# A hybrid encoder layer on one core: the second softmax's factor on GpSimd, other planned waits in attention, and a gate tile in another stage

## The chip, the cores and the metric

The kernel runs on one core of a Trainium2 chip. Its engines are TensorE (PE for matmuls, PEld for the loading of the stationary operand), the Vector engine (DVE), ScalarE (ACT), GpSimd (POOL) and SyncE (SP), which issues the DMAs. Each works off its own instructions in order and waits for the others on semaphores. The metric is the device time of one execution in microseconds (us). Three runs of the kernel before took 886.32, 886.88 and 886.91 us; the median is 886.88.

## What is computed

One layer (DEPTH is 1) of an encoder over 512 tokens of width 1024, all in float32. Cut to what matters:

```python
h = rms_norm(x, norm1_g[l])
proj = h @ w_in[l]                      # 1024 x 7680
u_pool, aq, ak, av, rq, rf, rb, ri, rg, gate_pre = split_cols(proj)
y_pool = pool_mixer(u_pool, pool_w[l], pool_scale[l])   # windows 2, 4, 8, 16; then a 128x128 map per group
# differential attention, 4 heads, two score maps (c = 0, 1) per head:
s = einsum('bqhcd,bkhcd->bhcqk', q, k) * scale - slopes * abs(qpos - pos)
p = softmax(s, axis=-1)
a = p[:, :, 0] - lam * p[:, :, 1]
y_attn = rms_norm(einsum('bhqk,bkhe->bqhe', a, v), gain) * (1.0 - lambda_init)
y_rec = hgrn2_mixer(rq, rf, rb, ri, rg, ...)            # bidirectional gated recurrence
gates = sigmoid(gate_pre.reshape(B, S, 3, D_MODEL))
merged = (gates[:, :, 0] * (y_pool @ w_up_pool[l]) + gates[:, :, 1] * (y_attn @ w_up_attn[l])
          + gates[:, :, 2] * (y_rec @ w_up_rec[l]))
x = x + merged @ w_out[l]
h2 = rms_norm(x, norm2_g[l])
gu = h2 @ w_ffn_in[l]
x = x + (silu(gu[..., :FFN_HIDDEN]) * gu[..., FFN_HIDDEN:]) @ w_ffn_out[l]
return rms_norm(x, final_norm_g)
```

## The kernel before

Operands of the large products are split in a high and a low part (`whi`, `wlo`; `hT_hi`, `hT_lo`), and a product is three terms: high by high, low by high, high by low. A *job* is one such product, most often of a tile of 128 output columns with all 512 tokens: 24 matmuls of 128x512 in three groups of eight for a column tile of `w_in`, 12 for a column tile of an up projection. For a job the weights are loaded by SP (`raw`), cast on ScalarE (`whi`, L183) and the rest formed on the Vector engine (`wlo`, L184), ahead of time, in three rotating buffers.

The program runs stage by stage. In each, `Pipe.run` interleaves several streams: a stream yields ("w", t) to say that it wants to go on only after t us of planned TensorE time, or ("e", name, t) to wait for an event. The stream of jobs never waits and so fills every gap. This plan fixes the order of TensorE's instructions. On the other engines a scheduler places instructions by its own timing of the program, so their order can change with any edit; each engine then keeps that order on the chip.

The attention stage runs four `att_head` streams, the `pool_windows` stream and the jobs from the queries and keys of attention to the four `pool_job` tiles (u0 to u3), with the first four up tiles of the recurrent branch among them. A head treats four query blocks. `scores(i)` makes two 128x512 score maps on TensorE (tiles `rc<-k,q` and `rc<-l,q`, four matmuls), adds the distances and finds the extreme on the Vector engine (L1056), takes the exponential with its sum on ScalarE (L1058, sums in `zz`), and forms on the Vector engine both reciprocals (`rr`, L1062), the factor `co` = -lam times the first sum over the second (L1064; `nlam` is -lam) and the weighted row `s` (L1066). `turn(i)` transposes that row on TensorE (L98, `tp<-ident,s`) and splits it (`aT_hi` on ScalarE, `aT_lo` on the Vector engine, L1076). After the fourth block come the product with the values (`rc<-aT_hi,va_hi` and so on, 12 matmuls) and `head_norm`: squares on ScalarE, four small products with ones (`tp<-onesD,sqo`), three small steps `mo` on the Vector engine with `rr`, a power on GpSimd (`rso`, L140), a product with `rr` (L667) and four transposes of `rso`. TensorE meets, in this order: scores(0), wait, scores(1), wait, turn(0), wait, scores(2), wait, turn(1), and so on.

`pool_windows` forms the pooled differences of u0 to u3 (`win`, L1159, and `gate`, L1166 and L1168). The next stage runs `pool_mix` (four groups: `dhi` on ScalarE, `dlo` on the Vector engine, L1181, three matmuls `rc<-dhi,pwhi`, `rc<-dlo,pwhi`, `rc<-dhi,pwlo`, an evacuation to `y_arena`), `SplitForms.stream` (sums of parts of h for later products, `gsum`, `ghi`, `glo`), and the jobs: gate tiles 4 and 5 of the recurrent branch (`add_gates((4, 5), "extra")`), its up tiles 4 and 5, gate tiles 6 and 7. A gate job ends with a sigmoid on ScalarE into a tile of `GATE[extra]`; an up job with a product `merged<-mm,gate` (L756).

Of the kernel before, what the change touches and what calls it, by code (L numbers as in the profile page):

```python
# [11 lines left out]
F32 = mybir.dt.float32  # L12
# [3 lines left out]
ALU = mybir.AluOpType  # L16
PSUM = bass.MemoryType.PSUM

P = 128
S = 512  # L20
D = 1024
NB = S // P
# [16 lines left out]
class Pipe:  # L39
# [8 lines left out]
    def mark(self, name):  # L48
        self.events[name] = self.t
# [27 lines left out]
def encoder_kernel(ctx: ExitStack, tc: tile.TileContext, x, norm1_g, w_in, pool_w, pool_scale,  # L77
# [3 lines left out]
    nc = tc.nc  # L81
# [3 lines left out]
    def pool(name, bufs=1, **kw):  # L85
        return tc.tile_pool(name=name, bufs=bufs, **kw)
# [21 lines left out]
    const = ctx.enter_context(pool("const"))  # L108
    wraw = ctx.enter_context(pool("wraw", 2))
    wsp = ctx.enter_context(pool("wsp", 3))  # L110
    small = ctx.enter_context(pool("small", 5))
# [15 lines left out]
    nc.vector.memset(onesD, 1.0 / P)  # L127
    mhalf = const.tile([P, 8], F32, name="mhalf")
    nc.vector.memset(mhalf, -0.5)
    masks = const.tile([P, len(LEVELS), P], U8, name="masks")  # L130
    vcol = const.tile([P, 14], F32, name="vcol")
    gain_a = const.tile([P, 1], F32, name="gain_a")
# [373 lines left out]
    GATE = {}  # L506
# [140 lines left out]
    def head_norm(o_ps, tmp, gain, r0=None, bufs=2):  # L647


        og = tmp.tile([P, S], F32, name="og", bufs=bufs)  # L650
        sq = tmp.tile([P, S], F32, name="sqo", bufs=bufs)
        nc.scalar.activation(out=sq, in_=o_ps, func=AF.Square)
        nc.scalar.activation(out=og, in_=o_ps, func=AF.Copy, scale=gain)
        yield ("w", 1.3)
        sp = bank("tp")
        for b in range(NB):
            mm(sp[:, b:b + 1], sq[:, b * P:(b + 1) * P], onesD, True, True)
        r = small.tile([P, NB], F32, name="rso")
        if r0 is None:
            rsqrt_eps(r, sp[:, 0:NB])  # L660
        else:
            m = small.tile([P, NB], F32, name="mo")
            nc.vector.tensor_tensor(out=m, in0=sp[:, 0:NB], in1=r0, op=ALU.mult)
            nc.vector.tensor_tensor(out=m, in0=m, in1=r0, op=ALU.mult)
            nc.vector.tensor_scalar(out=m, in0=m, scalar1=EPS, scalar2=None, op0=ALU.add)
            pow_mhalf(r, m)
            nc.vector.tensor_tensor(out=r, in0=r, in1=r0, op=ALU.mult)  # L667
        yield ("w", 3.55)
        rb = bank("tp")
        for b in range(NB):  # L670
            transpose(rb[:, b * P:(b + 1) * P], r[:, b:b + 1].to_broadcast([P, P]), ident)
        return og, rb
# [359 lines left out]
    def att_head(h):  # L1032
        if h:
            yield ("e", f"QK{h - 1}", 0.0)
        if h > 1:
            yield ("e", f"AN{h - 2}", 0.0)
        yield ("e", f"AF{h}", 6.0)
        t = att.pop(h)
        at, (vh, vl), aT, y_attn = ATT["at"], ATT["v"], ATT["aT"], ATT["y"]
        strip = ATT["strip"].tile([P, 896], F32, name="strip")  # L1040
        nc.sync.dma_start(out=strip, in_=c_dist[h])
        zz = at.tile([P, NB, 2], F32, name="zz")
        rr = at.tile([P, NB, 2], F32, name="rr")
        probs = {}

        def scores(i):
            bs = slice(i * P, (i + 1) * P)
            mx = small.tile([P, 2], F32, name="mx")
            ex = []
            for c in range(2):  # L1050
                ps = bank("rc")
                mm(ps, t[f"q{c}"][:, bs], t[f"k{c}"], True, False)
                mm(ps, t[f"q{c}"][:, bs], t[f"l{c}"], False, True)
                s = at.tile([P, S], F32, name=f"s{c}")

                nc.vector.tensor_tensor_reduce(out=s, in0=strip[:, 384 - P * i:896 - P * i], in1=ps, scale=1.0,  # L1056
                                               scalar=3.0e38, op0=ALU.add, op1=ALU.min, accum_out=mx[:, c:c + 1])
                nc.scalar.activation(out=s, in_=s, func=AF.Exp, scale=-1.0, bias=mx[:, c:c + 1],  # L1058
                                     accum_out=zz[:, i, c:c + 1])
                ex.append(s)  # L1060

            nc.vector.reciprocal(out=rr[:, i, :], in_=zz[:, i, :])  # L1062
            co = small.tile([P, 1], F32, name="co")
            nc.vector.scalar_tensor_tensor(out=co, in0=zz[:, i, 0:1], scalar=nlam, in1=rr[:, i, 1:2],  # L1064
                                           op0=ALU.mult, op1=ALU.mult)
            nc.vector.scalar_tensor_tensor(out=ex[0], in0=ex[1], scalar=co, in1=ex[0], op0=ALU.mult, op1=ALU.add)  # L1066
            probs[i] = ex[0]

        def turn(i):
            bs = slice(i * P, (i + 1) * P)  # L1070
            p = probs.pop(i)
            pt = bank("tp", (P, NB, P))
            for k in range(NB):
                transpose(pt[:, k, :], p[:, k * P:(k + 1) * P], ident)
            nc.scalar.copy(out=aT[0][:, :, bs], in_=pt)
            nc.vector.tensor_tensor(out=aT[1][:, :, bs], in0=pt, in1=aT[0][:, :, bs].bitcast(F32), op=ALU.subtract)  # L1076

        scores(0)
        for i in range(NB):
            yield ("w", 1.8 + (0.7 if i == 0 else 0.0))  # L1080
            if i + 1 < NB:
                scores(i + 1)
            else:
                mark(f"QK{h}")
            yield ("w", 1.6 + (1.0 if i + h == 0 else 0.0))
            if h and i == 0:
                yield ("e", f"PV{h - 1}", 0.0)
            turn(i)
        mark(f"T{h}")
        yield ("e", "VA", 1.5)  # L1090
        yield ("w", 1.5)
        ps = bank("rc")
        es = slice(h * P, (h + 1) * P)
        terms = [(vh, aT[0]), (vl, aT[0]), (vh, aT[1])]
        for i, (a, r) in enumerate(terms):
            for k in range(NB):
                mm(ps, a[:, k, es], r[:, k, :], i == 0 and k == 0, i == 2 and k == NB - 1)
            yield
        mark(f"PV{h}")
        og, rbp = yield from head_norm(ps, at, gain_a, rr[:, :, 0], 1)  # L1100
        mark(f"AN{h}")
        nc.vector.tensor_tensor(out=og, in0=og, in1=rbp, op=ALU.mult)
        nc.scalar.copy(out=y_attn[0][:, h, :], in_=og)
        nc.vector.tensor_tensor(out=y_attn[1][:, h, :], in0=og, in1=y_attn[0][:, h, :].bitcast(F32),
                                op=ALU.subtract)
# [32 lines left out]
    def add_pool(gs):  # L1138
        for g in gs:
            jobs.add([next(cols["u"])], pool_job(g))  # L1140

    add_pool((0, 1))
    br_rec.add_ups(range(2, 4))
    add_pool((2, 3))
    n_att = len(jobs.jobs)


# [24 lines left out]
    def pool_mix():  # L1172
        w, whi, wlo = POOL["w"], POOL["whi"], POOL["wlo"]
        nc.scalar.copy(out=whi, in_=w)
        nc.vector.tensor_tensor(out=wlo, in0=w, in1=whi.bitcast(F32), op=ALU.subtract)
        for g in range(4):
            yield ("w", 4.0)
            d = POOL[g][:, PAD:PAD + S]
            hi, lo = (POOL["t"].tile([P, S], F32R, name=n) for n in ("dhi", "dlo"))
            nc.scalar.copy(out=hi, in_=d)  # L1180
            nc.vector.tensor_tensor(out=lo, in0=d, in1=hi.bitcast(F32), op=ALU.subtract)  # L1181
            yield ("w", 2.6)
            ps = bank("rc")
            for i, (w_, r) in enumerate(((whi, hi), (whi, lo), (wlo, hi))):
                mm(ps, w_[:, g, :], r, i == 0, i == 2)
            y = POOL["y"]
            nc.scalar.activation(out=y[0][:, g, :], in_=ps, func=AF.Copy, scale=pscale[:, g:g + 1])
            nc.vector.scalar_tensor_tensor(out=y[1][:, g, :], in0=ps, scalar=pscale[:, g:g + 1],
                                           in1=y[0][:, g, :].bitcast(F32), op0=ALU.mult, op1=ALU.subtract)
            if g == 1:  # L1190
                mark("M1")

    br_rec.add_gates((4, 5), "extra")
    br_rec.add_ups((4, 5))
    br_rec.add_gates((6, 7), None, "M1")
    n_forms = len(jobs.jobs)
# [504 lines left out]
    stR.close()  # L1701

    merged.grow(stA.enter_context(pool("mp")))
    ya = stA.enter_context(pool("ya"))
    with ExitStack() as st:
        ap1 = st.enter_context(pool("ap1"))
# [20 lines left out]
    with ExitStack() as st:  # L1727
        pp = st.enter_context(pool("pp"))
        POOL["t"] = st.enter_context(pool("pt3"))
        GATE["extra"] = st.enter_context(pool("gp2", 2))  # L1730
        POOL["w"] = pp.tile([P, 4, P], F32, name="pw")
        POOL["whi"], POOL["wlo"] = (pp.tile([P, 4, P], F32R, name=n) for n in ("pwhi", "pwlo"))
        nc.sync.dma_start(out=POOL["w"], in_=pool_w[0].rearrange("g c d -> c g d"))
        forms = LAST["gforms"].stream(fm, st.enter_context(pool("gwork", 3)))
        pipe.run([pool_mix(), forms, jobs.stream(n_forms - n_att)])
# [95 lines left out]
```

## Time and profile before

| | us |
|---|---|
| profiled execution, device time | 886.27 |
| its span (first to last instruction) | 884.5 |
| Vector engine busy | 664.5 |
| ScalarE busy | 448.4 |
| GpSimd busy | 18.7 |
| start and end of the attention stage's blocks (first `s` row to last) | 220.2 to 329.6 |

A row of the timeline gives the start from the beginning of the span, the duration, the engine, the line of the kernel, the operation, what it writes and reads, its shape and the number of instructions merged in the row; in brackets the idle time of the engine before it and what ended that. A row of windows gives the stretch, its length, the busy time of each engine with its number of instructions, the granted clock of TensorE (1.00 is full), the DMA share and GB/s. A row of groups gives line, engine, operation and tile, then busy time, the mean duration in ns, and idle time before with what ended it.

### The profile page before, as it was taken

The numbers are of one execution on the slowest core, as the hardware profiler recorded it, in microseconds if no ns is written. First come the engines' busy times: TensorE is split into PE (matmuls) and PEld (weight loads), VectorE is DVE, ScalarE is ACT, GpSimd is POOL, SyncE is SP. The second block draws the span as 40 slices with busy tenths as digits, with TensorE's granted clock in tenths as the row PEclk, the third lists the DMA queues.
The fourth block names the chain that finished last, engine by engine and source line by source line (L and its number), as shares of the span: only waits on it lengthen the run. The fifth ranks groups of instructions, "written<-read, shape, count | busy, mean of one in ns | idle before, by whom it ended". The sixth has DMA issues, their size and how long they took to land.

```text
span 884.5 us, 14079 instructions
## 1 busy us (share of the span) xinstructions
PE 867.9 (98%) x5713; PEld 786.7 (89%) x5713; DVE 664.5 (75%) x1005; ACT 448.4 (51%) x718; POOL 18.7 (2%) x35
## 2 busy tenths in 40 slices
PE   8999999999999989999999999999999999999996
PEld 7989988888998867899999898999999999988885
DVE  6788664844857876987877555998888888747996
ACT  6544343434746743553455334755555655533463
POOL 1000000000000000000000001000000000000001
PEclk9999999999999999999999999999999999999999
DMA  8330113024123311334331770153443443355002
GB/s 243 96 120 24 49 48 116 27 73 141 49 88 94 94 61 49 96 96 137 101 97 48 262 191 1 49 143 96 125 115 96 123 118 97 119 190 189 2 1 96
DMA packets 115693, 87.53 MB, mean 99 GB/s; under 512 B 3862, under 2 KB 104748, under 8 KB 115628
## 3 DMA queue, kind: packets, MB, share of 16 engines
q1 hardware_dynamic: 115036, 85.57, 32.0%
q8 instruction: 45, 0.74, 0.3%
q10 hardware_dynamic: 592, 1.05, 0.3%
q14 instruction: 20, 0.16, 0.1%
HBM read 84.52 MB, written 2.10 MB: 98 GB/s over the span
## 4 chain that ended last, share of the span: by engine, by line
PE 87%; DVE 7%; DMA 2%; issue 1%; ACT 1%; POOL 0%; SPq 0%; POOLq 0%; DVEq 0%; ACTq 0%
PE mm L90 58%; PE rc L90 26%; PE tp L90 2%; PE tp L98 1%; DVE wlo L184 1%; DMA raw<-in_w_out_dram 1%; DMA raw<-in_w_in_dram 1%; DVE hid L354 1%; DVE flo L354 1%; DMA xin<-in_x_dram 0%; DVE s L1066 0%; DVE win L1159 0%; DVE hrow L481 0%; DVE h_lo L498 0%; PE rc L98 0%
## 5 line engine op out<-in xcount | busy, mean ns | idle before, releaser
L183 ACT CAST whi<-raw 128x1024 fp32r<-128x1024 f32 (+1 forms) x134 | 127.5, 958 | 138.4 <-PE mm L90 88.6
L184 DVE TENSOR_TENSOR wlo<-raw,whi 128x1024 fp32r<-128x1024 f32 (+1 forms) x134 | 147.6, 1106 | 58.2 <-ACT whi L183 35.5
L90 PE MATMUL mm<-hT_hi,whi 128*128 128x512 f32 (+1 forms) x344 | 82.1, 371 | 0.0
L90 PE MATMUL mm<-hT_hi,wlo 128*128 128x512 f32 (+1 forms) x344 | 81.7, 370 | 0.2 <-DVE wlo L184 0.2
L90 PE MATMUL mm<-hT_lo,whi 128*128 128x512 f32 (+1 forms) x344 | 81.5, 372 | 0.0
L302 DVE TENSOR_TENSOR slo<-sums,shi 128x1024 fp32r<-128x1024 f32 x58 | 70.5, 1218 | 0.2 <-ACT shi L300 0.2
L90 PEld LDWEIGHTS mm<-hT_lo,whi 128*128 128x128 f32 x344 | 60.0, 191 | 9.9
L90 PEld LDWEIGHTS mm<-hT_hi,whi 128*128 128x128 f32 x344 | 58.9, 189 | 9.9 <-ACT hT_hi L494 0.4
L90 PEld LDWEIGHTS mm<-hT_hi,wlo 128*128 128x128 f32 x344 | 58.5, 188 | 9.5 <-DVE wlo L184 0.4
L300 ACT CAST shi<-sums 128x1024 fp32r<-128x1024 f32 x58 | 61.0, 1053 | 4.1 <-DVE sums L264 3.7
L261 DVE TENSOR_TENSOR sums<-raw 128x1024 f32<-128x1024 f32 x29 | 35.4, 1219 | 1.7 <-DMA raw<-in_w_in_dram 1.6
L90 PE MATMUL mm<-y_arena,whi 128*128 128x512 f32 x128 | 32.8, 394 | 0.0
L90 PE MATMUL mm<-whi,y_arena 128*128 128x256 f32 (+1 forms) x192 | 31.9, 315 | 0.4 <-ACT whi L183 0.2
L914 DVE TENSOR_TENSOR kq<-kq,pyr 128x256 f32<-128x256 f32 x48 | 18.2, 421 | 18.2 <-PE rc L90 18.2
L90 PE MATMUL rc<-kq,kc 128*128 128x128 f32 x224 | 31.6, 284 | 0.0
L90 PEld LDWEIGHTS rc<-kq,kc 128*128 128x128 f32 x224 | 30.1, 191 | 1.5
L1058 ACT ACTIVATE s<-s,mx 128x512 f32<-128x512 f32 x32 | 23.0, 720 | 16.7 <-DVE mx L1056 16.5
L90 PEld LDWEIGHTS mm<-whi,y_arena 128*128 128x128 f32 x192 | 27.4, 188 | 3.5 <-ACT whi L183 1.0
L883 ACT COPY kc<-kq 128x512 f32<-128x512 f32 x28 | 18.6, 666 | 20.2 <-PE rc L90 12.6
L90 PEld LDWEIGHTS mm<-y_arena,whi 128*128 128x128 f32 x128 | 23.7, 188 | 5.1
L1346 DVE TENSOR_TENSOR g<-mm,g 128x256 f32<-128x256 f32 x21 | 8.9, 424 | 23.7 <-PE mm L90 23.7
L90 PE MATMUL mm<-fhi,slo 128*128 128x256 f32 x168 | 26.1, 277 | 0.5 <-DVE slo L302 0.5
(383 smaller groups left out, 2031.5 us busy)
## 6 DMA issues: line engine op xcount, KB each, us to landing
raw<-in_w_in_dram SPq DMA_DIRECT2D x44, 512.0 KB, 4.2
raw<-in_w_ffn_in_dram SPq DMA_DIRECT2D x44, 512.0 KB, 5.3
raw<-in_w_in_dram SPq DMA_DIRECT2D x8, 1024.0 KB, 5.2
raw<-in_w_ffn_out_dram SPq DMA_DIRECT2D x7, 1024.0 KB, 5.0
raw<-in_w_out_dram SPq DMA_DIRECT2D x4, 1024.0 KB, 11.1
xin<-in_x_dram SPq DMA_DIRECT2D x4, 512.0 KB, 4.6
raw<-in_w_up_rec_dram SPq DMA_DIRECT2D x2, 1024.0 KB, 6.4
raw<-in_w_up_pool_dram SPq DMA_DIRECT2D x2, 1024.0 KB, 5.1
```

Of the source, the lines that this page charges most:

```text
L90: i = nc.tensor.matmul(out_, lhsT=lhsT, rhs=rhs, start=start, stop=stop, skip_group_check=chain)
L98: tc.keep_in_program_order(nc.tensor.transpose(out_, in_, idn))
L183: nc.scalar.copy(out=hi, in_=view)
L184: LAST["wlo"] = nc.vector.tensor_tensor(out=lo, in0=view, in1=hi.bitcast(F32), op=ALU.subtract).ins
L261: nc.vector.tensor_tensor(out=strided(sums, 0, [[2 * half, 2], [1, half]]), in0=strided(self.raw, 0, [[3 * half, 2], [1, half]]), in1=stri ...
L300: nc.scalar.copy(out=hi, in_=view)
L302: on_dve = nc.vector.tensor_tensor(out=lo, in0=view, in1=hi.bitcast(F32), op=ALU.subtract).ins
L354: last[0] = form(**kw).ins
L883: nc.scalar.copy(out=strided(kc, 0, [[2 * n, S // (2 * n)], [n, 2], [1, n]]), in_=strided(kq, 2 * S, [[2 * n, S // (2 * n)], [S + n, 2], [ ...
L914: nc.vector.tensor_tensor(out=xv, in0=xv, in1=tv, op=ALU.mult)
L1058: nc.scalar.activation(out=s, in_=s, func=AF.Exp, scale=-1.0, bias=mx[:, c:c + 1], accum_out=zz[:, i, c:c + 1])
L1346: on_dve = nc.vector.tensor_tensor(out=c["g"], in0=c["x"], in1=c["g"], op=ALU.add).ins
```

## The change

It does four things.

1. *The factor.* Reciprocal and factor of each block leave the Vector engine. GpSimd forms `zn` = first sum times -lam, `co` = second sum to the power -1, and `co` times `zn`. The reciprocal of the first sums, which the head norm needs, is taken once per head for all four blocks.
2. *The waits.* In `att_head` 1.8 becomes 1.6 and 1.6 becomes 2.4; in `pool_mix` 4.0 becomes 2.0 and 2.6 becomes 3.6.
3. *The gate tile.* Gate tile 4 of the recurrent branch becomes the last job of the attention stage instead of the first of the next one; it gets its own pool, and gate tile 5 another.
4. Every engine but TensorE is scheduled anew as a result; lines behind L130 move by 2 to 5.

```diff
+    minus1 = const.tile([P, 1], F32, name="minus1")
+    nc.vector.memset(minus1, -1.0)
...
-        rr = at.tile([P, NB, 2], F32, name="rr")
+        rr = at.tile([P, NB], F32, name="rr")
...
-            nc.vector.reciprocal(out=rr[:, i, :], in_=zz[:, i, :])
-            co = small.tile([P, 1], F32, name="co")
-            nc.vector.scalar_tensor_tensor(out=co, in0=zz[:, i, 0:1], scalar=nlam, in1=rr[:, i, 1:2],
-                                           op0=ALU.mult, op1=ALU.mult)
+            zn, co = (small.tile([P, 1], F32, name=n) for n in ("zn", "co"))
+            nc.gpsimd.tensor_tensor(out=zn, in0=zz[:, i, 0:1], in1=nlam, op=ALU.mult)
+            nc.gpsimd.tensor_tensor(out=co, in0=zz[:, i, 1:2], in1=minus1, op=ALU.pow)
+            nc.gpsimd.tensor_tensor(out=co, in0=co, in1=zn, op=ALU.mult)
             nc.vector.scalar_tensor_tensor(out=ex[0], in0=ex[1], scalar=co, in1=ex[0], op0=ALU.mult, op1=ALU.add)
...
-            yield ("w", 1.8 + (0.7 if i == 0 else 0.0))
+            yield ("w", 1.6 + (0.7 if i == 0 else 0.0))
             if i + 1 < NB:
                 scores(i + 1)
...
-            yield ("w", 1.6 + (1.0 if i + h == 0 else 0.0))
+            yield ("w", 2.4 + (1.0 if i + h == 0 else 0.0))
...
         mark(f"T{h}")
+        nc.vector.reciprocal(out=rr, in_=zz[:, :, 0])
...
-        og, rbp = yield from head_norm(ps, at, gain_a, rr[:, :, 0], 1)
+        og, rbp = yield from head_norm(ps, at, gain_a, rr, 1)
...
     add_pool((2, 3))
+    br_rec.add_gates((4,), "4")
...
-            yield ("w", 4.0)
+            yield ("w", 2.0)
...
-            yield ("w", 2.6)
+            yield ("w", 3.6)
...
-    br_rec.add_gates((4, 5), "extra")
+    br_rec.add_gates((5,), "5")
...
+    GATE["4"] = stA.enter_context(pool("gp4"))
...
-        GATE["extra"] = st.enter_context(pool("gp2", 2))
+        GATE["5"] = st.enter_context(pool("gp5"))
```

What it moves is shown at three places. The first is TensorE at the end of attention, from the scores of the last block (head 3, query block 3) to its transposes; `y_arena` are the up tiles 2 and 3 of the recurrent branch, `hT` the tile u2. Before:

```order
L90 MATMUL rc<-k_2757,q_2755 128x512
L90 MATMUL rc<-l_2759,q_2755 128x512
L90 MATMUL rc<-k_2758,q_2756 128x512
L90 MATMUL rc<-l_2760,q_2756 128x512
L90 MATMUL mm<-y_arena,whi 128x512 x2
L90 MATMUL mm<-y_arena,wlo 128x512 x4
L90 MATMUL mm<-y_arena,whi 128x512 x2
L98 MATMUL tp<-ident,s_3066 128x128 x4
L90 MATMUL mm<-y_arena,whi 128x512 x6
L90 MATMUL mm<-y_arena,wlo 128x512 x4
L90 MATMUL mm<-hT_hi,whi 128x512 x8
L98 MATMUL tp<-ident,s_3125 128x128 x4
```

The change:

```order
L90 MATMUL rc<-k_2765,q_2763 128x512
L90 MATMUL rc<-l_2767,q_2763 128x512
L90 MATMUL rc<-k_2766,q_2764 128x512
L90 MATMUL rc<-l_2768,q_2764 128x512
L90 MATMUL mm<-y_arena,whi 128x512 x8
L90 MATMUL mm<-y_arena,wlo 128x512 x4
L98 MATMUL tp<-ident,s_3106 128x128 x4
L90 MATMUL mm<-hT_hi,whi 128x512 x8
L90 MATMUL mm<-hT_lo,whi 128x512 x8
L90 MATMUL mm<-hT_hi,wlo 128x512 x4
L98 MATMUL tp<-ident,s_3171 128x128 x4
```

Between the scores and the transposes of the block (`s_3125`, now `s_3171`) stood 26 matmuls of 128x512 and the transposes of the block before; now 32 and those transposes. Behind the last up tile (`y_arena`) stood eight matmuls, now the transposes of the block before and 20 matmuls.

The second is the Vector engine at the same place, from the product of the last up tile (`merged`) to the last block's weighted row; `wlo` belongs to gate tile 4, `pwlo` to the pooling weights, `gate` is the pooled difference of u1. Before:

```order
L756 TENSOR_TENSOR merged<-mm,gate 128x512
L1166 SCALAR_TENSOR_TENSOR win<-win,rcnt 128x2x8
L184 TENSOR_TENSOR wlo<-raw,whi 128x1024
L1064 SCALAR_TENSOR_TENSOR co<-zz,nlam,rr 128x1
L1175 TENSOR_TENSOR pwlo<-pw,pwhi 128x512
L1168 SCALAR_TENSOR_TENSOR gate<-win,gate 128x512
L1066 SCALAR_TENSOR_TENSOR s_3125<-s_3131,co,s_3125 128x512
```

The change:

```order
L758 TENSOR_TENSOR merged<-mm,gate 128x512
L1133 MEMSET gate 128x8
L1134 MEMSET gate 128x8
L1172 SCALAR_TENSOR_TENSOR gate<-win,gate 128x512
L186 TENSOR_TENSOR wlo<-raw,whi 128x1024
L1179 TENSOR_TENSOR pwlo<-pw,pwhi 128x512
L1078 TENSOR_TENSOR aT_lo<-tp,aT_hi 128x4x128
L1068 SCALAR_TENSOR_TENSOR s_3171<-s_3177,co,s_3171 128x512
```

The factor is gone from the row of the queue, the small edge product `win` stands earlier, the edges of u3 are cleared here (L1133, L1134), and the split of the block before (`aT_lo`) has come in.

The third is TensorE from the transposes of the last head's norm (`rso`) to the first mixing matmul of the next stage; `hT` are the end of u3 and the gate tiles 4 and 5. Before:

```order
L98 MATMUL tp<-ident,rso 128x128 x4
L90 MATMUL mm<-hT_hi,wlo 128x512 x6
L90 MATMUL mm<-hT_hi,whi 128x512 x8
L90 MATMUL mm<-hT_lo,whi 128x512 x8
L90 MATMUL mm<-hT_hi,wlo 128x512 x8
L90 MATMUL mm<-hT_hi,whi 128x512 x8
L90 MATMUL mm<-hT_lo,whi 128x512 x2
L90 MATMUL rc<-dhi,pwhi 128x512
```

The change:

```order
L98 MATMUL tp<-ident,rso 128x128 x4
L90 MATMUL mm<-hT_hi,whi 128x512 x2
L90 MATMUL mm<-hT_lo,whi 128x512 x8
L90 MATMUL mm<-hT_hi,wlo 128x512 x8
L90 MATMUL mm<-hT_hi,whi 128x512 x8
L90 MATMUL mm<-hT_lo,whi 128x512 x8
L90 MATMUL mm<-hT_hi,wlo 128x512 x8
L90 MATMUL mm<-y_arena,whi 128x512 x4
L90 MATMUL rc<-dhi,pwhi 128x512
```

Of the transposes' place: six matmuls of u3 and all 24 of gate tile 4 came behind it, now 18 of gate tile 4. The first mixing group stood inside gate tile 5 and now stands inside up tile 4. From these transposes to the third mixing group there were 114 matmuls of 128x512, now 100.

## The prediction

> **What bounds the kernel now.** I read the page first (busy time, the 40 slices), then the waits of TensorE in the attention stage, then the timeline around each of them.
>
> ```profile
> span 884.5 us, 14079 instructions
> PE 867.9 (98%) x5713; PEld 786.7 (89%) x5713; DVE 664.5 (75%) x1005; ACT 448.4 (51%) x718; POOL 18.7 (2%) x35
> PE   8999999999999989999999999999999999999996
> ```
>
> TensorE is the bound, and both kernels have the same matmuls. So a change of the order can only win back what TensorE loses: its idle time, and time at a lower clock. Besides the first and the last slice only one slice drops to 8: the 15th, at 310 to 332 us, where attention ends. The waits of TensorE from 203 to 348 us are three in all (total, times, longest):
>
> ```profile
> PE tp L98 <- DVE s L1066: 2.8, 1, 2.8
> PE tp L98 <- DVE rr L1062: 1.0, 1, 1.0
> PE tp L98 <- DVE rso L667: 0.6, 1, 0.6
> ```
>
> So of the 16 blocks (four heads, four query blocks each) 14 had their weighted row `s` ready when TensorE came to turn it; two had not, and one head norm was late. In the timeline (start, duration, engine, work):
>
> ```profile
> 311.25 0.63 PE L98 MATMUL tp<-ident,s 128*128 128x128 f32 x4 [1.01 <-DVE rr L1062]
> 329.75 1.09 PE L98 MATMUL tp<-ident,s 128*128 128x128 f32 x4 [2.79 <-DVE s L1066]
> 330.49 3.06 PE L90 MATMUL mm<-hT_lo,whi 128*128 128x512 f32 x8
> 333.39 1.08 PE L90 MATMUL rc<-aT_hi,va_hi 128*128 128x512 f32 x4
> 343.69 0.62 PE L98 MATMUL tp<-ident,rso 128*128 128x128 f32 x4 [0.56 <-DVE rso L667]
> ...
> 203.45 1.98 PE L90 MATMUL mm<-hT_lo,whi 128*128 128x512 f32 x8
> 205.26 1.98 PE L90 MATMUL mm<-hT_hi,wlo 128*128 128x512 f32 x8
> ...
> 316.90 0.44 PE tp L98 x4
> ...
> 310.00:320.00 10.00, 8.99 (x48) 7.49 (x48) 6.93 (x19) 5.40 (x13) 1.01 (x1) 1.00 0.00 0
> 329.60:333.40 3.80, 3.65 (x13) 3.12 (x14) 0.69 (x2) 0.59 (x1) 0.00 (x0) 0.61 0.00 0
> ```
>
> Eight matmuls take 205.26 - 203.45 = 1.81 us, so 0.226 us each, and four transposes 0.44 us in the chain. Behind the hole of 2.79 us the same four transposes and eight matmuls took 333.39 - 329.75 = 3.64 us instead of 2.25: 1.39 us lost to a granted clock of 0.61 there (the hole of 1.01 us left it at 1.00). The stage's loss is 2.79 + 1.39 + 1.01 + 0.56 = **5.75 us**. That is the most the change can win.
>
> **The waits: more matmuls in front of the transposes.** From the scores of a block to its transposes the plan had 1.6 + 1.8 + 1.6 = 5.0 us of TensorE time, now 2.4 + 1.6 + 2.4 = 6.4. As built, the last block has 32 matmuls and one group of transposes between, before 26 and one: 6 x 0.226 = 1.36 us more cover. By the same count twelve blocks gain 1.36 us or more, two gain 0.7 and 0.9, and two lose 0.7 and 1.8 of covers of 18 us and more. No matmul is added.
>
> **The last block.** What was late there is the Vector engine's queue, not the factor:
>
> ```profile
> 324.68 0.19 ACT L1058 ACTIVATION_READ_ACCUMULATOR s<-s,mx 128x1 f32 x1
> 324.98 1.98 PE L90 MATMUL mm<-hT_hi,whi 128*128 128x512 f32 x8
> 325.71 0.68 DVE L756 TENSOR_TENSOR merged<-mm,gate 128x512 f32<-128x512 f32 x1
> 326.39 1.22 DVE L184 TENSOR_TENSOR wlo<-raw,whi 128x1024 fp32r<-128x1024 f32 x1
> 327.52 0.21 DVE L1064 SCALAR_TENSOR_TENSOR co<-zz,nlam,rr 128x1 f32<-128x1 f32 x1
> 327.65 0.68 DVE L1175 TENSOR_TENSOR pwlo<-pw,pwhi 128x512 fp32r<-128x512 f32 x1
> 328.26 0.68 DVE L1168 SCALAR_TENSOR_TENSOR gate<-win,gate 128x512 f32<-128x512 f32 x1
> 328.86 0.75 DVE L1066 SCALAR_TENSOR_TENSOR s<-s,co,s 128x512 f32<-128x512 f32 x1
> ```
>
> The second exponential was read at 324.87, and `s` ended at 329.61. Count from 324.98, where the second up tile's matmuls had been issued: `s` ended 4.63 us later, and TensorE was there after eight matmuls, 1.81 us. Now, from the same point, the Vector engine has merged, two memsets, gate, wlo, pwlo, aT_lo, s. By starts in these rows: 0.60 (merged) + 0.60 (gate) + 1.13 (wlo) + 0.61 (pwlo) + 0.61 (aT_lo, taken like pwlo) + 0.75 (s) = 4.3, with 0.1 for the memsets and 0.25 until the up tile can be read (a matmul of 0.39 us outlasts its issue by 0.16, a hand-over takes 0.1) 4.65 us: as late as before. But TensorE now has four transposes and 20 matmuls there, 0.44 + 4.52 = 4.96 us. So the 2.79 us close, and so does the clock's 1.39; the spare is 0.31 less the 0.14 us from the end of `s` to the transposes, 0.17. For a miss of this thin sum I charge 0.3 us.
>
> **The factor on GpSimd.** It removes 16 reciprocals and 16 products from the Vector engine and adds four reciprocals of 128x4; GpSimd gets 48 small operations.
>
> ```profile
> L1062 DVE RECIPROCAL rr<-zz 128x2 f32<-128x2 f32 x16 | 2.6, 162 | 5.1 <-ACT s L1058 4.9
> L1064 DVE SCALAR_TENSOR_TENSOR co<-zz,nlam,rr 128x1 f32<-128x1 f32 x16 | 3.5, 218 | 0.4
> L140 POOL TENSOR_TENSOR rstd<-ms,mhalf 128x1 f32<-128x1 f32 x8 | 4.4, 555 | 0.7
> L140 POOL TENSOR_TENSOR rso<-mo,mhalf 128x4 f32<-128x4 f32 x4 | 5.0, 1244 | 137.3 <-DVE mo L665 82.1 <-DVE win L1166 29.2 <-DVE co L1064 26.0
> L146 POOL TENSOR_SCALAR ms<-ss 128x1 f32<-128x1 f32 x8 | 1.9, 243 | 216.5 <-ACT hrow L475 216.5
> ```
>
> Old chain: 0.16 + 0.22 = 0.38 us and its steps. New: `zn` hides behind the second exponential; the power is that of the third row, 0.55 us. No row has a product of two 128x1 tiles on GpSimd: not under 0.19 (the shortest `ms`), not over the power's 0.55; I take 0.25, by the nearest row. With two more hand-overs of 0.1 the chain grows by 0.55 + 0.25 + 0.2 - 0.4 = 0.6 us, against 1.36 us of cover. The Vector engine saves 16 x 0.38 - 4 x 0.16 = 5.4 us of work beside TensorE: nothing on the path by itself, since TensorE waited three times only. Behind an `s` that waits for GpSimd stand the split and the `aT_lo` of the block before; both feed matmuls that come later than the transposes. On GpSimd the head norm's power may stand between `zn` and the factor, 1.0 us, in three of four heads.
>
> A GpSimd operation can also be held up by the Vector engine:
>
> ```profile
> 262.95 1.01 POOL L140 TENSOR_TENSOR rso<-mo,mhalf 128x4 f32<-128x4 f32 x1 [61.88 <-DVE mo L665]
> 283.96 0.75 DVE L1066 SCALAR_TENSOR_TENSOR s<-s,co,s 128x512 f32<-128x512 f32 x1
> 284.18 1.40 POOL L140 TENSOR_TENSOR rso<-mo,mhalf 128x4 f32<-128x4 f32 x1 [20.22 <-DVE mo L665]
> ...
> 553.22 0.55 POOL L140 TENSOR_TENSOR rstd<-ms,mhalf 128x1 f32<-128x1 f32 x1
> 553.25 0.70 DVE L264 TENSOR_TENSOR sums<-sums,raw 128x512 f32<-128x512 f32 x1
> ```
>
> The power begun beside a Vector operation with two inputs in SBUF took 1.40 us, not 1.01; the Vector operation begun just behind a power took its usual 0.70. So a start here costs GpSimd the rest of one Vector operation, 0 to 1.13 us, and the Vector engine nothing. The four powers of the norms took 1.24 us on average, 0.23 more than a free one: three steps make 0.7, and the chain's growth is 0.6 to 1.3 us, still under 1.36.
> [...]
>
> **The other two holes.** At 311 us block 0 of the last head was 1.01 us late; it has 1.36 more cover, against 0.6: 0 to 0.4 us may stay, I take 0.1, as the block's exponentials now stand ahead of the norm's two passes on ScalarE. The 0.56 us belonged to a norm whose three small steps were mixed with pooling additions; now these stand ahead of the steps, in one piece, with the same matmuls in front of the transposes: closed.
>
> **The gate tile.** The matmuls are the same in the same sequence; its DMA keeps its place in SP's queue. What moves is the mixing matmuls behind it, and the Vector engine's sums for the next stage, which start by their plan:
>
> ```profile
> 348.00:400.00 52.00, 52.00 (x311) 45.94 (x311) 47.45 (x56) 30.20 (x41) 0.00 (x0) 1.00 0.31 91
> 348.17 3.49 DVE L387 TENSOR_TENSOR gsum<-hT_hi,hT_lo 128x1024 f32<-128x1024 f32 x3
> 367.24 0.69 DVE L1181 TENSOR_TENSOR dlo<-gate,dhi 128x512 fp32r<-128x512 f32 x1
> 370.14 0.39 PE L90 MATMUL rc<-dhi,pwhi 128*128 128x512 f32 x1
> ```
>
> TensorE had no hole there, and the Vector engine was nearly full. From the last norm's transposes (343.69) the third mix came after 26.45 us, its `dlo` was ready after 24.2: spare 2.2. Of the matmuls between 100 are left of 114, since 12 of the gate tile's stand ahead now and two more have changed sides: 14 x 0.226 = 3.2 us, so the mix comes after 23.3. `dlo` moves as well: three pooling additions go ahead of the sums, two evacuations of earlier mixes come in (0.61 each), and the sums start 0.7 us sooner behind the transposes, since a split of weights goes ahead: 24.2 - 1.8 + 1.2 - 0.7 = 22.9. Spare 0.4, unsure by 0.7: I charge 0.2 us.
>
> **Sum.** 886.27 (the profiled run; its span is 884.5, 1.8 lie around it) - 5.75 + 0.3 + 0.1 + 0.2 = 881.1 us. That run lies 0.6 us under the median of 886.88, so I add 0.1: **881.2**.
>
> **Rivals.**
> 1. *The last block stays late.* If `s` comes 1.4 us later (GpSimd held by wlo for 1.13 and a slower product), the hole of 1.4 stays, and the clock may fall again: 881.2 + 1.4 + 1.39 = 884.0; a full 2.79 + 1.39 gives 885.4. For it: eight operations in one queue. Against: its two up tiles are now done earlier.
> [...]
> 2. *The next stage takes the wait.* The Vector engine is its bound; a `dlo` or a sum late by 1 to 3 us gives 882 to 884.
> 3. *The change doesn't do what it says:* the factor is later on GpSimd by as much as the waits add, and small holes of 0.3 to 0.5 us at a dozen blocks replace the three: 885.2 to 887.
> 4. *Slower: GpSimd held up at each of its three steps.* A free block shows the spare:
>
> ```profile
> 319.46 0.75 DVE L1066 SCALAR_TENSOR_TENSOR s<-s,co,s 128x512 f32<-128x512 f32 x1
> 322.23 0.60 PE L98 MATMUL tp<-ident,s 128*128 128x128 f32 x4
> ```
>
> It had 322.23 - 320.21 = 2.0 us. With 1.36 it stands a growth of 3.4; 0.6 + 3 x 1.13 = 4.0 passes that, by 0.6 us at 13 blocks, 8 us: 888.5. It decides from a chain longer by 3.4 us. Against it: the average hold is 0.23, a fifth of 1.13.
>
> **How the numbers follow.** Forecast 0.57 (880.5 to 882.5), rival 1 0.15, rival 2 0.12, rival 3 0.10, rival 4 0.06. A difference of 0.2%, 1.8 us, is about what a measurement of this kernel can tell from no change. Faster: 0.57 + 0.12 + two thirds of 0.15 = 0.79; same 0.05 + 0.10 = 0.15; slower 0.06. The range runs from 879.9 (all won, 880.5, less the 0.6 us by which the three runs differ) to 885.0, which leaves out rivals 3 and 4 and the end of rival 1.
>
> **What would show it.** Right: no wait of TensorE on `s` or `rso` over 0.5 us in attention, granted clock 1.00 there, GpSimd busy for 18.7 + 17 us. Wrong: a wait of `tp` on `s` at several blocks (rival 3 or 4), one of 1 us or more at the last block (1), a wait of `rc` on `dlo` (2). Should most of the 5.75 us come back outside attention, the sum was wrong in its premise that only these holes count.

## The result, and the profile after

The changed kernel takes 896.70 us (median of four runs, 896.43 to 897.97) against 886.89 for the kernel before: a ratio of 1.0114, 95% interval 1.0096 to 1.0131. It is slower by 9.8 us; 881.2 was forecast. One execution of a variant below, the gate tile alone, took 1298.42 us at a granted clock of 0.63 and is left aside; it is the profiled one of that variant, which is therefore judged by its time alone. Yet what the forecast says of attention came about. The page of the changed kernel begins so (busy time of the engines with their instructions, then the granted clock in 40 slices):

```profile
span 894.6 us, 14114 instructions
PE 882.1 (99%) x5713; PEld 794.5 (89%) x5713; DVE 661.3 (74%) x978; ACT 449.3 (50%) x718; POOL 36.4 (4%) x83
PEclk9999999999999999999999999999999999999999
```

TensorE has the same 5713 matmuls, but it is busy for 14.2 us longer (867.9 before). The time did not come as waiting and not as a lower clock. Of its waits from 203 to 348 us (total, times, longest) these are left, and none is one of the three holes:

```profile
PE rc L90 <- ACT l L1025: 0.4, 1, 0.4
PE tp L98 <- POOL rso L142: 0.3, 1, 0.3
```

The windows of that stretch (length, busy time of PE, PEld, DVE, ACT, POOL, then the clock), first of the kernel before, then of the changed one:

```profile
203.00:348.00 145.00, 140.50 (x758) 120.01 (x757) 100.00 (x222) 83.98 (x158) 4.98 (x4) 0.99 0.28 88
```

```profile
203.00:348.00 145.00, 144.30 (x777) 122.21 (x776) 99.47 (x199) 86.00 (x160) 23.20 (x53) 1.00 0.28 88
```

Here the changed kernel does 19 matmuls more. It loses in stretches in which no line of the change works. Windows of TensorE at 600 to 700 us, far behind attention, in the kernel before and in the changed one:

```profile
600.00:700.00 100.00, 100.00 (x885) 1.00 0.43 117
```

```profile
600.00:700.00 100.00, 100.00 (x861) 1.00 0.38 106
```

TensorE is busy for all of the 100 us at full clock in both, and the changed kernel does 24 matmuls fewer there (the mix of lengths in the two windows is not quite the same, so this is a sign and not a measure). Ahead of attention it is the same. The timeline of TensorE at 41 us, in the kernel before:

```profile
40.97 1.98 PE L90 MATMUL mm<-hT_lo,whi 128*128 128x512 f32 x8
42.78 0.61 PE L90 MATMUL mm<-hT_hi,wlo 128*128 128x512 f32 x2
```

and in the changed kernel:

```profile
41.12 2.04 PE L90 MATMUL mm<-hT_lo,whi 128*128 128x512 f32 x8
43.00 0.63 PE L90 MATMUL mm<-hT_hi,wlo 128*128 128x512 f32 x2
```

From start to start the eight matmuls take 1.81 us before and 1.88 now: 0.226 and 0.235 us each. Not all matmuls became slower. Groups of TensorE in the second half (busy, mean ns), before:

```profile
L90 PE MATMUL mm<-fhi,shi 128*128 128x256 f32 x168 | 26.0, 277 | 0.1
L90 PE MATMUL mm<-fhi,whi 128*128 128x256 f32 x84 | 13.1, 277 | 0.1
```

and after:

```profile
L90 PE MATMUL mm<-fhi,shi 128*128 128x256 f32 x168 | 26.0, 277 | 0.0
L90 PE MATMUL mm<-fhi,whi 128*128 128x256 f32 x84 | 13.6, 283 | 0.0
```

The same moving tile `fhi` costs the same with the weights `shi`, and 6 ns more with the weights `whi`. What tells `shi` from `whi` is where they lie. The two new tiles, `minus1` in `const` and `zn` in `small`, are 4 bytes in each partition, but all tiles behind them in the memory move: those behind `const` by 32 bytes, those behind `small` by 192 (of that 160 for the five buffers of `zn`). By the addresses that the two programs give their tiles, in bytes modulo 256:

| tile | before | after |
|---|---|---|
| `whi`, `wlo` (split weights, three buffers) | 32 | 64 |
| `hT_hi`, `hT_lo` | 32 | 224 |
| `fhi`, `flo` | 224 | 160 |
| `shi` read with `fhi` | 32 | 224 |

`fhi` and `shi` moved together, by 192 bytes; `fhi` and `whi` did not, nor did `hT` and `whi`. So the theory to test is **place**: the bytes at which the two operands of a matmul start set its pitch. The rival is **work**: GpSimd's 48 new operations or the new order slow TensorE.

### The profile page after: what moved, and what is told of

Same layout as the page of the kernel before. It is cut to its first block, busy times and chain, and to the rows that moved or that the text cites. A ratio compares the mean times of both kernels' runs of the same rounds, so it can differ in the third digit from the quotient of the medians.

```text
span 894.6 us, 14114 instructions
## 1 busy us (share of the span) xinstructions
PE 882.1 (99%) x5713; PEld 794.5 (89%) x5713; DVE 661.3 (74%) x978; ACT 449.3 (50%) x718; POOL 36.4 (4%) x83
## 4 chain that ended last, share of the span: by engine, by line
PE 86%; issue 7%; DMA 3%; DVE 2%; ACT 1%; POOL 1%; SPq 0%; POOLq 0%; DVEq 0%; ACTq 0%
PE mm L90 56%; PE rc L90 26%; PE tp L90 2%; PE tp L98 2%; DMA raw<-in_w_in_dram 1%; DMA raw<-in_w_out_dram 1%; DVE wlo L186 1%; DMA xin<-in_x_dram 0%; ACT whi L185 0%; ACT s L1060 0%; POOL rso L142 0%; PE rc L98 0%; DVE hrow L483 0%; ACT l L1025 0%; DVE slo L304 0%
## 5 line engine op out<-in xcount | busy, mean ns | idle before, releaser
L90 PE MATMUL mm<-hT_hi,whi 128*128 128x512 f32 (+1 forms) x344 | 84.0, 375 | 0.0
```

The source lines that it names most:

```text
L90: i = nc.tensor.matmul(out_, lhsT=lhsT, rhs=rhs, start=start, stop=stop, skip_group_check=chain)
```

## Experiments

**Place against work.** In the first run the changed kernel keeps its work, and its tiles get their old bytes modulo 256 back:

```diff
-    onesD = const.tile([P, 1], F32, name="onesD")
+    onesD2 = const.tile([P, 2], F32, name="onesD")
+    onesD, minus1 = onesD2[:, 0:1], onesD2[:, 1:2]
...
-    minus1 = const.tile([P, 1], F32, name="minus1")
...
-            zn, co = (small.tile([P, 1], F32, name=n) for n in ("zn", "co"))
+            cz = small.tile([P, 2], F32, name="co")
+            zn, co = cz[:, 0:1], cz[:, 1:2]
```

> The changed kernel with its two new small tiles put into spare bytes of old ones (the constant -1 beside onesD, zn beside co), so that every tile that TensorE reads starts at the same byte modulo 256 as in the kernel before. Theory 'place': the 32 and 192 bytes by which the new tiles push all tiles behind them set the pitch of the matmuls; here the pitch is 0.226 us again (8 matmuls 203.45 to 205.26 took 1.81), PE busy falls from 882.1 to about 868, and the time is the one that was predicted, 881.2 (879.9 to 885.0). Rival 'work': the new GpSimd work or the new order slows the matmuls; then nothing changes, 896 to 897.

It took **881.37 us** (ratio 0.9947, 0.9927 to 0.9967, against 886.84 on the same chip), with PE busy for 867.1 us. The second is the kernel before with two unused tiles of those sizes; `pad` is a helper that the kernel before has, which allocates a tile that nothing reads or writes:

```diff
     nc.vector.memset(mhalf, -0.5)
+    pad(const, 4, "const_a")
...
     small = ctx.enter_context(pool("small", 5))
+    pad(small, 160, "small_a")
```

> The kernel before with two unused tiles and nothing else: 32 bytes where the changed kernel puts -1, 160 bytes where it puts zn, so that its tiles up to the attention stage and behind it start where the changed kernel's do. 'Place': PE busy rises by the 14.2 us that the changed kernel's rose (867.9 to 882.1) and the time to about 901, with the attention stage's three waits as before. 'Work': 886.9, as before.

It took **901.51 us** (1.0170, 1.0151 to 1.0190). Its three holes in attention stay (2.6, 1.0 and 0.5 us). So 192 bytes that nobody reads cost the old kernel 14.7 us, and the changed one owes 896.70 - 881.37 = 15.3 us to them. Work is out.

**Which operand.** Two more versions of the changed kernel: one with 64 more unused bytes behind `small`, so that modulo 256 only the split weights stand at a new place, and one in which only the rest does.

```diff
+    pad(small, 64, "small_a")
```

> The changed kernel with 64 further unused bytes behind the small tiles: the weights that were split (whi, wlo) stay 32 bytes behind their old place, everything from hT on is 256 bytes behind it, and so at the same byte modulo 256 as before. 'Place', if the distance of the moving operand counts or the moving operand alone: 881 to 884; if the place of the weights alone counts: 896. 'Work': 896.

```diff
-    onesD = const.tile([P, 1], F32, name="onesD")
+    onesD2 = const.tile([P, 2], F32, name="onesD")
+    onesD, minus1 = onesD2[:, 0:1], onesD2[:, 1:2]
...
-    minus1 = const.tile([P, 1], F32, name="minus1")
...
+    pad(small, 32, "small_a")
```

> The opposite of the run before: the weights whi and wlo at their old bytes, everything from hT on 192 bytes behind, as in the changed kernel. 'Place', if the moving operands (hT and what lies behind it) count: about 896; if the place of the split weights alone: 881 to 884. 'Work': 896.

They took 896.53 us (1.0115, 1.0096 to 1.0135) and 893.24 us (1.0075, 1.0052 to 1.0098). My two readings, "the weights' place" and "the moving tile's place", are both wrong as each stood: to move either is nearly as bad as to move both. That is how a distance behaves. The timeline of TensorE at the same eight matmuls, first with only the weights moved:

```profile
40.87 2.03 PE L90 MATMUL mm<-hT_lo,whi 128*128 128x512 f32 x8
42.73 0.63 PE L90 MATMUL mm<-hT_hi,wlo 128*128 128x512 f32 x2
```

then with only `hT` and what lies behind it:

```profile
40.96 2.03 PE L90 MATMUL mm<-hT_lo,whi 128*128 128x512 f32 x8
42.83 0.63 PE L90 MATMUL mm<-hT_hi,wlo 128*128 128x512 f32 x2
```

1.86 and 1.87 us, 0.2325 and 0.2338 each.

**The cost by itself.** Eight moving tiles and eight weight tiles, all pairs, TensorE alone, in one profiled execution:

```python
m = [mv.tile([P, 520], F32R, name="m" + c) for c in "abcdefgh"]   # each starts 32 bytes further modulo 256
w = [wt.tile([P, 264], F32R, name="w" + c) for c in "abcdefgh"]
...
tc.keep_in_program_order(nc.tensor.matmul(o[:, :n], lhsT=w[j][:, a:a + 128], rhs=m[i][:, :n], ...))  # a: 0, 128, 0, ...
```

> Nothing of the reference is computed: 8 moving tiles ma to mh and 8 weight tiles wa to wh, each starting 32 bytes further modulo 256 than the one before (a at 128, e at 0, f at 32), and 16 matmuls of 128x512 and 16 of 128x256 for each of the 64 pairs, with every other engine idle. Theory 'TensorE's own two reads' (the distance between moving tile and weights sets the pitch): the 64 pairs fall into classes, about 0.226 and 0.240 us for 128x512, 0.113 and 0.120 us for 128x256, and the class follows from the distance modulo 64, 128 or 256. Theory 'one tile alone': the class follows from the row or the column. Rival 'other engines' (their reads and writes collide with TensorE's, and the place only decides how): all 64 pairs alike.

The timeline of this run, for the moving tile `md` (it starts at 224) with all eight weights, and a second pair of equal places, `mf` and `wf` (both at 32); each row is 16 matmuls:

```profile
121.88 3.90 PE L61 MATMUL full<-md,wa 128*128 128x512 f32 x16
125.62 3.84 PE L61 MATMUL full<-md,wb 128*128 128x512 f32 x16
129.30 3.89 PE L61 MATMUL full<-md,wc 128*128 128x512 f32 x16
133.02 3.80 PE L61 MATMUL full<-md,wd 128*128 128x512 f32 x16
136.66 3.89 PE L61 MATMUL full<-md,we 128*128 128x512 f32 x16
140.38 3.90 PE L61 MATMUL full<-md,wf 128*128 128x512 f32 x16
144.12 3.90 PE L61 MATMUL full<-md,wg 128*128 128x512 f32 x16
147.86 3.88 PE L61 MATMUL full<-md,wh 128*128 128x512 f32 x16
...
199.87 3.80 PE L61 MATMUL full<-mf,wf 128*128 128x512 f32 x16
203.51 3.89 PE L61 MATMUL full<-mf,wg 128*128 128x512 f32 x16
```

From start to start, over 16: `md` with `wd`, both at 224, 3.64 us, or 0.2275 us a matmul; `mf` with `wf`, both at 32, 3.64 as well. `md` with `we` (32 further) 3.72, `wf` (64 further) 3.74, `wg` (96 further) 3.74. The program gives the other engines only the copies that fill the 16 tiles, and the output behind the matmuls, and after the first start at 9.24 us no pair shows idle time of TensorE; so what differs from pair to pair is its two operands. Over the pairs of 128x512 (but the first and the last, whose rows do not give it) those of one distance agree to within 0.002 us: 0.2275 at 0, with one pair at 0.2294; 0.230 at 192; 0.232 to 0.234 at the other six. Row or column alone decides nothing, and the two classes of 0.226 and 0.240 that were expected are not there. Set against the kernels, at the eight matmuls of `hT_lo` and `whi` (distance: start of the weights less start of the moving tile, modulo 256):

| kernel | `hT`, `whi` start at | distance | here, us a matmul | in the kernel |
|---|---|---|---|---|
| before | 32, 32 | 0 | 0.2275 | 1.81 / 8 = 0.226 |
| only weights moved | 32, 64 | 32 | 0.2325 | 0.2325 |
| only the rest moved | 224, 32 | 64 | 0.2338 | 0.2338 |
| changed kernel | 224, 64 | 96 | 0.2338 | 0.235 |

The distance gives the four pitches to within 0.0015 us. With 256 columns the spread is wider, and one distance is not one pitch. In the same run, two pairs with the weights 64 bytes further than the moving tile:

```profile
308.14 1.98 PE L61 MATMUL half<-mc,we 128*128 128x256 f32 x16
309.96 2.09 PE L61 MATMUL half<-mc,wf 128*128 128x256 f32 x16
311.88 2.05 PE L61 MATMUL half<-mc,wg 128*128 128x256 f32 x16
...
325.16 2.05 PE L61 MATMUL half<-md,wf 128*128 128x256 f32 x16
327.05 2.04 PE L61 MATMUL half<-md,wg 128*128 128x256 f32 x16
```

`mc` with `we` takes 1.82 us, 0.114 each; `md` with `wf`, at the same distance, 1.89, 0.118; and `mc` with `wf`, at distance 96, 1.92, 0.120. What decides between 0.114 and 0.118 stays open.

**Distance against place, in the whole kernel.** The changed kernel with its new tiles left where they are, and everything else, at both ends of the memory, moved to 32 bytes behind its old place modulo 256:

```diff
-    pad(ctx.enter_context(pool("top", side="right")), 192, "top")
+    pad(ctx.enter_context(pool("top", side="right")), 160, "top")
...
+    pad(small, 96, "small_a")
```

> The changed kernel with its two new tiles where they are, and everything that TensorE reads moved to 32 bytes behind its old place modulo 256: 96 unused bytes behind the small tiles, 32 fewer at the other end of the memory. Absolute places are all new, the distances between moving tiles and weights are those of the kernel before. If the distance counts: 881 to 882.5, with 0.226 us for a 128x512 matmul of hT. If the place itself counts (as that of the weights, 32 bytes off, could in the runs before): 896.

**881.51 us** (0.9941, 0.9922 to 0.9960). Timeline of TensorE:

```profile
41.44 1.98 PE L90 MATMUL mm<-hT_lo,whi 128*128 128x512 f32 x8
43.25 0.61 PE L90 MATMUL mm<-hT_hi,wlo 128*128 128x512 f32 x2
```

1.81 us again, with the split weights at 64 as in the slow kernels. The distance counts.

**The parts of the change, with the places held.** From the first run (881.37) one part at a time is undone: the factor back on the Vector engine, the old waits, the old gate tiles.

> The kernel of the first run (places held) with the factor back on the Vector engine (reciprocal of 128x2 and product at each block), new waits and new gate tile kept. If more matmuls in front of the transposes close the holes, as the prediction has it: the same as with GpSimd, 881 to 882. If it is the factor's move that closes them: 2.8 us and a low clock at the last block again, 885 to 887.

> Places held, factor on GpSimd, gate tile as in the changed kernel, but the old waits (1.8 and 1.6, 4.0 and 2.6): 26 matmuls and one group of transposes in front of the last block again. If the waits close the holes: the three holes stay, longer by the 0.6 to 1.3 us by which the factor's chain grew, 886.5 to 889. If the factor does: 881 to 882.

> Places held, factor on GpSimd and new waits, but both gate tiles behind the stage as before. The prediction charged the gate tile's move 0.2 us in the stage behind attention: 881 to 882 here. If the move itself wins or loses something: over 1 us away from the 881.4 of the first run.

They took 881.27 (0.9950, 0.9935 to 0.9966), 881.80 (0.9956, 0.9939 to 0.9973) and 881.31 us (0.9952, 0.9935 to 0.9969), against 886.23 on that chip. The old waits came out against the prediction: without the new ones nothing is lost that the time can tell. So the parts were run alone on the kernel before, the factor (with `minus1` and `zn` in spare bytes), the four waits, the gate tile:

> The kernel before with the factor on GpSimd alone, places held; old waits, old gate tiles. The order of the Vector engine's queue at the last block (weighted row in front of the split of weights, as in the run with the old waits) should come from this part alone: 881.5 to 883, the last block's hole under 1 us. If the gate tile was needed for it: 885 to 887.

> The kernel before with the four new waits alone. If more matmuls in front of the transposes are enough by themselves: 881 to 882. If they need the factor on GpSimd or the gate tile inside the stage: 884 to 887.

> The kernel before with the gate tile alone as the attention stage's last job. It adds no matmul in front of the last block's transposes and moves nothing on the Vector engine ahead of the weighted row: the three holes stay, 886 to 887.5. If it does more than that: 882 to 884.

881.76 (0.9947, 0.9928 to 0.9967), **881.09** (0.9937, 0.9918 to 0.9957) and 886.82 us (1.0001, 0.9990 to 1.0012), against 886.71 on that chip. Factor and waits win 4.95 and 5.62 us alone; the gate tile wins nothing, by its time alone. How the factor does it stands in the timeline of the last block, in the run of the factor alone:

```profile
325.68 0.19 POOL L1068 TENSOR_TENSOR co<-co 128x1 f32<-128x1 f32 x1
326.54 0.74 DVE L1069 SCALAR_TENSOR_TENSOR s<-s,co,s 128x512 f32<-128x512 f32 x1
327.20 1.22 DVE L186 TENSOR_TENSOR wlo<-raw,whi 128x1024 fp32r<-128x1024 f32 x1
327.43 0.63 PE L98 MATMUL tp<-ident,s 128*128 128x128 f32 x4 [0.39 <-DVE s L1069]
```

In the kernel before, `wlo`, `pwlo` and `gate` stood ahead of `s` on the Vector engine, and so did its own small `co`, behind `wlo`. With the factor on GpSimd the scheduler has `s` ahead of `wlo`: a hole of 0.39 us where 2.79 were, without one matmul more in front. That the small `co` alone held `s` behind `wlo` is argued and not shown. The factor does not close everything: of the waits of TensorE from 203 to 348 us these are left in the same run, the first at 311 us, where 1.01 us were lost before:

```profile
PE tp L98 <- DVE mo L666: 1.0, 1, 1.0
PE tp L98 <- DVE s L1069: 0.4, 1, 0.4
```

The run with only the waits undone has the same two. With the waits alone `wlo` and `pwlo` still stand ahead of `s` on the Vector engine, and `gate` and a split of the block before as well, but TensorE comes later:

```profile
325.30 1.22 DVE L184 TENSOR_TENSOR wlo<-raw,whi 128x1024 fp32r<-128x1024 f32 x1
326.47 0.68 DVE L1175 TENSOR_TENSOR pwlo<-pw,pwhi 128x512 fp32r<-128x512 f32 x1
327.97 0.75 DVE L1066 SCALAR_TENSOR_TENSOR s<-s,co,s 128x512 f32<-128x512 f32 x1
328.87 0.63 PE L98 MATMUL tp<-ident,s 128*128 128x128 f32 x4
```

`s` ends at 328.72, and the transposes follow without a wait. Seven versions lie between 881.1 and 881.8 us and beat both kernels; they can't be told apart. The smallest is the four numbers of the waits.

## Why the prediction was wrong, step by step

**The step that failed is the premise**: "both kernels have the same matmuls. So a change of the order can only win back what TensorE loses: its idle time, and time at a lower clock". The matmuls are the same, their pitch is not. The 0.226 us of one place in the trace of before was carried into the changed kernel; there it is 0.235 for the same matmuls. With the other pairs that changed their distance this costs 896.70 - 881.37 = 15.3 us, against the 5.5 us that the rest of the change wins. The two tiles stood in the diff, and their effect on all addresses behind them could have been read from the two programs beforehand; no rival had it. A sign of it stood in the kernel before: seven `pad` tiles of 64 or 192 bytes, which hold nothing and can only move what lies behind them. The sentence kept for this case, that the premise is wrong should the time come back outside attention, names it.

The run with TensorE alone has 0.2275 and 0.2338 us for the same 128x512 matmul at two distances, 3% apart; with 256 columns the pairs run from 0.114 to 0.120, 5%. Why is not shown; the runs show only that with 512 columns the pitch goes with the distance between the operands. Nor do they tell whether the weights that count are the matmul's own or those loaded for the next one (PE and PEld are busy for 882.1 and 794.5 of 894.6 us in the changed kernel, so weights are loaded while matmuls run): within each of the rows above both start at the same byte modulo 256.

**The sum, apart from the premise**, was right: 881.2 forecast, 881.37 with the places held. That the two agree to 0.2 us is luck in part. The four executions run from 881.19 to 882.68; none of the charges of 0.3, 0.1 and 0.2 us came up as a wait, and two waits that no term had did, 0.6 us on `l` (of the matmuls `rc`) inside attention and 1.0 us more for a cast of weights behind attention (below).

- *The holes.* Closed as said, with the clock at 1.00. For the last block 4.65 us were forecast for `s` and 4.96 for TensorE, from the transposes before. In the changed kernel's timeline:

```profile
327.56 0.60 PE L98 MATMUL tp<-ident,s 128*128 128x128 f32 x4
...
329.50 1.12 POOL L1066 TENSOR_TENSOR co<-zz,minus 128x1 f32<-128x1 f32 x1 [1.82 <-ACT s L1060]
331.33 0.75 DVE L1068 SCALAR_TENSOR_TENSOR s<-s,co,s 128x512 f32<-128x512 f32 x1
332.67 0.60 PE L98 MATMUL tp<-ident,s 128*128 128x128 f32 x4
```

  `s` ended 332.08 - 327.56 = 4.52 us behind them, TensorE was there after 332.67 - 327.56 = 5.11. The longer pitch helps here a little: 20 matmuls at 0.235 are 0.18 us more than at 0.226.
- *What closes them.* "What was late there is the Vector engine's queue, not the factor": the queue it was, but its order changed when the factor's small operations left it. The prediction took the waits for the only cure; for the last block either part is one. The hole at 311 us is gone with the waits alone and stays at 1.0 us with the factor alone.
- *The factor's chain.* Of the terms 0.55 for the power and 0.25 for a product, the first was short. Groups of GpSimd in the changed kernel:

```profile
L1066 POOL TENSOR_TENSOR co<-zz,minus 128x1 f32<-128x1 f32 x16 | 11.3, 707 | 12.7 <-ACT s L1060 12.7
L1065 POOL TENSOR_TENSOR zn<-zz,nlam 128x1 f32<-128x1 f32 x16 | 3.9, 242 | 76.5 <-ACT s L1060 76.4
L1067 POOL TENSOR_TENSOR co<-co,zn 128x1 f32<-128x1 f32 x16 | 3.5, 221 | 1.3
```

  0.71 and 0.22, together 0.93 where 0.55 + 0.25 + up to 0.7 for holds was the span: inside. GpSimd's busy time rose by 36.4 - 18.7 = 17.7 us; 17 was said. Rival 4 did not come; its price does not add up as written (881.2 and 8 us are 889.2, not 888.5), and nothing else rests on it. Nor did a power on GpSimd hold up the Vector engine: a `wlo` begun at 320.85 us in the changed kernel, 0.02 us behind a power of 0.55, took 1.24 us, where the one shown in the prediction took 1.22.
- *The gate tile* was charged 0.2 us. With and without it, 881.37 and 881.31: too small to tell. Rival 2, the next stage taking a wait, did not come: with the places held none of TensorE's waits from 348 to 700 us is on `dlo`. Most of that waiting is for a cast of weights on ScalarE, 1.2 us in two waits where it was 0.2; TensorE is busy for 98.77 us from 400 to 500, where the kernel before had all 100. What made it longer is open.

```profile
PE mm L90 <- ACT whi L185: 1.2, 2, 1.0
```

## What to carry to other kernels

A small tile that is allocated ahead of the tiles TensorE reads is part of a change's cost (here 192 bytes that nobody reads cost 14.7 us): compare the start addresses of moving tiles and weights modulo 256 in the two programs before counting waits, and put new small tiles into spare bytes or behind the large ones. When all of TensorE's windows are full and hold fewer matmuls each (here 861 for 885 in 100 us), look at pitch, not at waits: time eight equal matmuls from start to start. Undo each part of a change alone and also run each alone: of two parts that close the same hole, each looks useless when it is undone (881.27 and 881.80 us here, 881.37 with both) and sufficient when it is run alone (881.76 and 881.09).

## What was not expected of the hardware

The pitch of a matmul went with the distance of its two operands in the memory, in a program that is TensorE's matmuls alone but for the filling of the tiles and the output: 0.2275 us at 0 bytes, 0.2325 at 32, 0.2338 at 64 and 96, 0.230 at 192 (modulo 256, 128x512). With 256 columns one distance had two pitches, 0.114 and 0.118. The kernels show it as well: with only the weights moved, `ghi` and `shi` start at the same bytes modulo 256 as before, and the group slows from 276 ns to 281. Groups of TensorE, in the kernel before and with only the weights moved:

```profile
L90 PE MATMUL mm<-ghi,shi 128*128 128x256 f32 x64 | 9.9, 276 | 0.0
```

```profile
L90 PE MATMUL mm<-ghi,shi 128*128 128x256 f32 x64 | 10.2, 281 | 0.0
```

So the distance modulo 256 is not the whole rule for short matmuls; what sets the second pitch was not settled. A power on GpSimd that was begun beside a two-input operation of the Vector engine took 1.12 us instead of 0.55 (at 329.50 above; `wlo` ran from 328.99 to 330.21).
